# A mixer of sparse and latent attention: group A's query projections between the heads of group B, the top-k block after block, index products and ropes in PSUM

## The chip, the cores and the metric

The kernel runs on one core of one Trainium2 chip. The metric is device time in microseconds of one launch. The core's engines are TensorE (PE), VectorE (DVE), ScalarE (ACT), GpSimd (POOL) and SyncE (SP), which issues the DMAs.

## What is computed

One decoder layer on 512 tokens of 1024 numbers, all in float32:

```python
x = x + 0.5 * swiglu(rmsnorm(x, g_ffn1), w1_gate, w1_up, w1_down)      # 1024 -> 2816 -> 1024
h = rmsnorm(x, g_mix)
qa, ka, va, qi, ki, wi, cq, ckv, kr = split(h @ w_in)
qa, ka, qi, ki = (rope(t) for t in (qa, ka, qi, ki))                   # kr and part of q likewise, below
# group A: an index of 16 heads scores every causal key, each query keeps 128
score = sum over h of wi[:, h] * relu(qi[:, h] @ ki.T)                 # causal
out_a = softmax(qa @ ka.T / 8 over the 128 best keys by score) @ va    # 8 heads, one shared key and value
# group B: latent attention, 8 heads, dense and causal
q = rmsnorm(cq, g_q_lat) @ w_uq; k, v = split(rmsnorm(ckv, g_kv_lat) @ w_ukv)
out_b = softmax(q @ [k, rope(kr)].T / sqrt(96)) @ v
x = x + concat(out_a, out_b) @ w_out
x = x + 0.5 * swiglu(rmsnorm(x, g_ffn2), w2_gate, w2_up, w2_down)
return rmsnorm(x, g_final)
```

## The kernel before

Every matmul that needs float32 is three: `mm3` (L135) multiplies the high part of the weights by the high and the low part of the data, and the low part of the weights by the high one (L137, L140, L141). `split` (L93) makes the parts: ACT copies the high one (L94), DVE or POOL subtracts it for the low one (L95). The two feed-forward layers use this with 128x512 tiles; they and their code stay as they are.

Between them stands `mixer` (L574). Tokens of the string `ORDER` (L27) name its steps, and the steps run in the string's order. Ahead of the bar come `q0` to `q7` (index query projections), `s` (their rope and the stack of four rows of high and low parts for the index product), `i0` to `i7` (two index heads each), `l0` to `l4` (the latents, with their norm), `K`, `R`, `V` (keys and values of group B), `p`, `u` (rotary queries of B), `A0` to `A3` with `S0` to `S3` (query projections of group A with rope and stack) and `b3` and the like (three rounds of the top-k). Behind the bar a unit of attention is four tokens: `g` gathers its operands, `s` makes the scores and the softmax, `z` divides by the sums, `a` transposes the probabilities and multiplies them by the values. Units 0 to 7 are the heads of B, 8 to 15 a query block of A each for two groups of four heads. `o0` to `o7` are the output projection. A second table, `ON_VECTOR` (L32), names the operations that go to DVE rather than POOL (`engine`, L395). The scheduler of the language orders each engine's instructions from this, by the operands' readiness.

What the steps issue:

- `rope` (L622) reads a projection from PSUM: DVE multiplies by the cosine (L626); the sine half is either two more on DVE (L628, L629) or an ACT copy (L632) and two on POOL (L633, L634); the sum is L635. The operands of all but the first are in SBUF. `stack` (L644) then copies to SBUF (L648, L650) and subtracts (L649).
- `index_heads` (L700): for each query block of 256, 384 and 512 keys two matmuls (L707, L708) into a PSUM bank, a relu by ACT into an SBUF tile r, four of which exist (L710), and DVE's multiply-add of r into the score tile `idx` (L711).
- `topk` (L715): 16 rounds; in each, for each of the three blocks, MAX8 (L719) finds the eight largest and MATCH_REPLACE (L720) overwrites them. At the end the taken are made a mask (L723).
- `softmax` (L862): DVE adds the mask and takes the maximum out of PSUM (L872), prepares the bias (L876, L878), ACT exponentiates (L880); `normalise` (L883) is a reciprocal (L887) and a product, on POOL (L890) or DVE (L892). The probabilities of a unit lie in one of three tiles.
- `Mla` (L910) for a head of B: scores L942 to L944, transposes L957, copies out of PSUM (L906 DVE, L908 ACT, in `taken`), values L960. `Dsa` (L965) does the same for A: L982, L983, L993, L998.
- All PSUM tiles come from one pool of eight banks (`ps`, L73). Transposed blocks have seven SBUF buffers (`ah=7`).

```python
for i in range(1, NT):                                    # L715, in each of 16 rounds
    m8 = small(8)
    nc.vector.max(out=m8, in_=score[i])
    nc.vector.match_replace(out=score[i], in_to_replace=m8, in_values=score[i], imm_value=TAKEN)
```

Of the kernel before, what the change touches and what calls it, by code (L numbers as in the profile page):

```python
# [25 lines left out]
BUFS = dict(pf=5, pr=4, ph=2, ah=7)  # L26
ORDER = """q0 q1 T c s0 r s1 t k q2 v w q3 i0 q4 a s2 i1 s4 q6 i2 q7 s3 q5 s6 s7 e s5 i3 l0 i4 i7 l1 i5 i6 l2 l3 l4 p b3 n0 u A0  # L27
A1 b2 K S0 A2 R b2 b2 S1 b2 A3 b3 S3 V S2 |
g0 s0 n1 g1 b2 g2 b2 s1 z0 s2 z1 b2 g3 g4 a0 s3 a1 b2 g5 z2 s4 a2 b2 z4 g6 z3 s5 g7 a3 s6 g8 z5 b2 b2 g9 a4 s7 g10 a5
b2 z6 s8 b2 a6 b2 b2 z7 a7 s9 o0 z8 g11 b2 b2 g12 b20 z9 b2 s10 z10 a8 s11 a9 a10 z11 g13 s12 o1 a11 g14 s13 z12 g15  # L30
s14 z13 s15 a12 z14 b2 o2 a13 a14 z15 a15 o3 o4 o5 b2 b2 o6 b2 o7 b2"""
ON_VECTOR = set("""c0.0 c0.1 c0.2 c0.3 c1.0 c1.2 c10.0 c11.0 c13.0 c14.3 c15.0 c15.1 c15.3 c2.1 c2.3 c3.1 c3.2 c3.3 c4.0 c4.3  # L32
c5.1 c6.0 c6.1 c6.2 c6.3 c7.2 gk5 gk7 kf mrA2 mrT mre mrq1 mrq2 mrq3 mrq5 mrq7 oa00 oa01 oa02 oa10 oa20 oa23
oa31 oa32 oa33 ob1 ob2 re rq1 rq2 rq3 rq5 ru1 sA2 sq6 sq7 su1 wA3 wV wl0 wl3 wo0 wo1 wo4 wo5 wo6 wo7 wq1 wq2
wq5 wq6 wq7 z0.0 z0.2 z0.3 z10.0 z10.2 z11.2 z12.0 z12.2 z12.3 z13.0 z13.2 z14.2 z14.3 z15.0 z15.1 z15.2 z2.3
z3.0 z3.1 z3.2 z3.3 z4.2 z4.3 z5.1 z5.2 z6.0 z6.2 z7.0 z7.1 z7.2 z7.3 z8.0 z9.0 z9.1""".split())
# [4 lines left out]
class Kernel:  # L41
    def __init__(self, ctx, tc):
# [8 lines left out]
        self.psp = pool("psp", space=bass.MemoryType.PSUM)  # L51
# [343 lines left out]
def engine(nc, name):  # L395

    return nc.vector if name in ON_VECTOR else nc.gpsimd


def add_mixer_weights(k, w_in, w_uq, w_ukv, w_out):  # L400
# [9 lines left out]
    lo = lambda name: engine(nc, "w" + name)  # L410
# [27 lines left out]
    def rope_chunk(col, *names):  # L438
# [25 lines left out]
    def plain(col, *names):  # L464
# [48 lines left out]
    def prep_pe():  # L513
        h, l = k.whl()
        for c in range(2):
            for half in range(2):
                hv, lv = (x[:, :768].rearrange("p (a g s h b) -> p a g s h b", a=3, g=2, s=2, h=4)[:, :, c, half]
                          for x in (h, l))
                k.split(hv, lv, uq[c][:, :, :, 64 + 16 * half:80 + 16 * half], lo("p"))
        return tuple(x[:, :768].rearrange("p (a g b) -> p a g b", a=3, g=2) for x in (h, l))  # L520

    def prep_nope(c):
        def f():
            h, l = k.whl()
            hv, lv = (x[:, :768].rearrange("p (a h b) -> p a h b", a=3, h=4) for x in (h, l))
            k.split(hv, lv, uq[c][:, :, :, 0:64], lo(f"n{c}"))
# [12 lines left out]
    for part in (1, 0):  # L539
        for half in range(2):  # L540
# [692 lines left out]
```

## Time and profile before

| | |
|---|---|
| device time, median of 3 runs | 1060.51 us (1060.31 to 1060.97) |
| the profiled execution's own time | 1061.52 us |
| its span in the trace | 1059.7 us |
| mean granted clock of PE | 0.987 |
| PE busy | 1016.4 us, 96% of the span |
| DVE busy | 513.2 us, 48% |
| ACT busy | 384.3 us, 36% |
| POOL busy | 147.5 us, 14% |

Busy time is the time in which an engine had an instruction in work. The shares are means over stages that differ: the feed-forward layers fill PE, the mixer in between, some 290 us of 1060, doesn't. The granted clock is the share of full speed that PE was given. A wait belongs to the engine that stands still; it is put down to the instruction that ended it last.

### The profile page before, as it was taken

The page shows a single profiled execution, that of the slowest core. Times are in us where ns is not written, and L with a number is a line of the kernel's source. Part 1 is how long each engine was busy: PE and PEld are TensorE (multiplying, and loading weights), DVE is VectorE, ACT ScalarE, POOL GpSimd, SP SyncE. Part 2 cuts the span into 40 slices and gives each one's busy share as a digit, 9 for nine tenths or more (in the row PEclk, how much of TensorE's full clock was granted, in tenths as well). Part 3 has the DMA queues.
Part 4 walks back from the last instruction along what each step waited for, and adds up shares of the span by engine and source line. Part 5 has one row for each costly group of instructions (what it writes and reads, how often), then busy time and mean ns, then how long its engine had stood idle before and what let it go on. Part 6 is the DMA issues. An engine that isn't in the chain of part 4 may idle for free.

```text
span 1059.7 us, 12214 instructions
## 1 busy us (share of the span) xinstructions
PE 1016.4 (96%) x4726; PEld 829.8 (78%) x4726; DVE 513.2 (48%) x897; ACT 384.3 (36%) x689; POOL 147.5 (14%) x142
## 2 busy tenths in 40 slices
PE   6999999999999999889879999999999999999997
PEld 4888888888888888768755567888888888888886
DVE  6433333233332346989996767553333233333343
ACT  5422222122222335563466556442222211222232
POOL 1000000000000026625975122000000000000000
PEclk9999999999999999989988999999999999999999
DMA  8322332233313123333350001344323232222302
GB/s 278 120 80 81 118 119 80 80 99 109 111 60 97 40 80 109 114 92 98 98 174 15 2 19 43 102 138 124 113 80 119 80 113 86 80 83 98 119 0 80
DMA packets 83390, 98.84 MB, mean 93 GB/s; under 512 B 9026, under 2 KB 65474, under 8 KB 83332
## 3 DMA queue, kind: packets, MB, share of 16 engines
q1 hardware_dynamic: 83328, 98.06, 29.4%
q8 instruction: 37, 0.61, 0.2%
q14 instruction: 21, 0.17, 0.1%
q10 hardware_dynamic: 4, 0.00, 0.0%
HBM read 91.89 MB, written 2.10 MB: 89 GB/s over the span
## 4 chain that ended last, share of the span: by engine, by line
PE 80%; DVE 12%; issue 3%; ACT 3%; POOL 1%; DMA 1%; SPq 0%; POOLq 0%; ACTq 0%; DVEq 0%
PE ps L137 24%; PE ps L140 24%; PE ps L141 24%; DVE idx L720 2%; DVE s L719 2%; DVE idx L711 1%; PE ps L960 1%; DVE wl L95 1%; PE ps L998 1%; DVE p L892 1%; PE ps L993 1%; PE ps L957 1%; DVE p L872 1%; PE ps L982 1%; DVE f L626 0%
## 5 line engine op out<-in xcount | busy, mean ns | idle before, releaser
L94 ACT ACTIVATE wh<-raw 128x1024 fp32r<-128x1024 f32 (+4 forms) x154 | 140.1, 925 | 381.1 <-PE ps L140 298.9
L95 DVE TENSOR_TENSOR wl<-raw,wh 128x1024 fp32r<-128x1024 f32 (+1 forms) x122 | 145.5, 1196 | 266.2 <-ACT wh L94 265.9
L137 PE MATMUL ps<-xh,wh 128*128 128x512 f32 (+2 forms) x712 | 265.9, 378 | 5.1 <-DVE res L1137 1.7
L141 PE MATMUL ps<-xh,wl 128*128 128x512 f32 (+2 forms) x712 | 267.3, 377 | 1.2 <-POOL wl L95 0.9
L140 PE MATMUL ps<-xh,wh 128*128 128x512 f32 (+2 forms) x712 | 267.2, 377 | 0.5 <-DVE xh L95 0.5
L137 PEld LDWEIGHTS ps<-xh,wh 128*128 128x128 f32 x712 | 133.7, 189 | 29.6 <-DVE f L629 2.1
L141 PEld LDWEIGHTS ps<-xh,wl 128*128 128x128 f32 x712 | 134.6, 189 | 24.9 <-POOL wl L95 1.3
L140 PEld LDWEIGHTS ps<-xh,wh 128*128 128x128 f32 x712 | 134.5, 189 | 23.6 <-DVE xh L95 0.7
L137 PE MATMUL ps<-wh,h 128*128 128x512 f32 x272 | 105.9, 389 | 0.0
L140 PE MATMUL ps<-wl,h 128*128 128x512 f32 x272 | 105.8, 389 | 0.0
L141 PE MATMUL ps<-wh,h 128*128 128x512 f32 x272 | 105.8, 389 | 0.0
L95 POOL TENSOR_TENSOR wl<-raw,wh 128x512 fp32r<-128x512 f32 (+5 forms) x32 | 43.3, 1374 | 394.4 <-ACT wh L94 389.8
L334 DVE TENSOR_TENSOR t<-ps,t 128x512 f32<-128x512 f32 x44 | 30.4, 691 | 138.5 <-PE ps L141 138.5
L94 ACT ACTIVATE w<-raw 128x1024 fp32r<-128x1024 f32 x32 | 33.9, 1061 | 117.5 <-PE ps L140 117.5
L137 PE MATMUL ps<-xh,w 128*128 128x512 f32 x176 | 68.5, 389 | 0.0
L141 PE MATMUL ps<-xh,w 128*128 128x512 f32 x176 | 68.5, 389 | 0.0
L140 PE MATMUL ps<-xh,w 128*128 128x512 f32 x176 | 68.5, 389 | 0.0
L289 POOL TENSOR_TENSOR fr<-tot,mhalf 128x1 f32<-128x1 f32 x12 | 7.0, 582 | 417.9 <-DVE tot L1180 360.1
L140 PEld LDWEIGHTS ps<-wl,h 128*128 128x128 f32 x272 | 51.1, 188 | 10.6
L141 PEld LDWEIGHTS ps<-wh,h 128*128 128x128 f32 x272 | 51.1, 188 | 10.6
L137 PEld LDWEIGHTS ps<-wh,h 128*128 128x128 f32 x272 | 51.0, 188 | 10.6
L95 DVE TENSOR_TENSOR w<-raw,w 128x1024 fp32r<-128x1024 f32 x32 | 39.2, 1225 | 29.8 <-ACT w L94 29.8
(214 smaller groups left out, 1346.2 us busy)
## 6 DMA issues: line engine op xcount, KB each, us to landing
raw<-in_w_up_dram SPq DMA_DIRECT2D x22, 1024.0 KB, 5.3
raw<-in_w_gate_dram SPq DMA_DIRECT2D x21, 1024.0 KB, 5.3
raw<-in_w_down_dram SPq DMA_DIRECT2D x20, 1024.0 KB, 5.0
raw<-in_w_in_dram SPq DMA_DIRECT2D x8, 1024.0 KB, 5.2
raw<-in_w_out_dram SPq DMA_DIRECT2D x4, 1024.0 KB, 5.8
res<-in_x_dram SPq DMA_DIRECT2D x4, 512.0 KB, 6.0
raw<-in_w_down_dram SPq DMA_DIRECT2D x4, 512.0 KB, 3.8
raw<-in_w_ukv_dram SPq DMA_DIRECT2D x2, 1024.0 KB, 4.9
```

The source lines that it names most:

```text
L94: i = self.nc.scalar.activation(hi, src, AF.Copy)
L95: (lo_engine or self.nc.vector).tensor_tensor(out=lo, in0=src, in1=hi.bitcast(F32), op=ALU.subtract)
L137: i = mm(out, wh, xh, start=first, stop=False)
L140: mm(out, wh, xl, start=False, stop=False)
L141: return i, mm(out, wl, xh, start=False, stop=last)
L334: nc.vector.tensor_tensor(out=u, in0=pu, in1=g, op=ALU.mult)
L711: nc.vector.scalar_tensor_tensor(out=score[i], in0=r, scalar=wt[:, i, h:h + 1], in1=cm(i) if h == 0 else score[i], op0=ALU.mult, op1=ALU.add)
L719: nc.vector.max(out=m8, in_=score[i])
L720: nc.vector.match_replace(out=score[i], in_to_replace=m8, in_values=score[i], imm_value=TAKEN)
L872: nc.vector.tensor_tensor_reduce(out=e, in0=p[:, :n], in1=bias, scale=1.0, scalar=-3.0e38, op0=ALU.add, op1=ALU.max, accum_out=mx[:, c:c + 1])
L892: nc.vector.tensor_scalar(out=e, in0=e, scalar1=rc[:, c:c + 1], scalar2=None, op0=ALU.mult)
L957: nc.tensor.transpose(p[:, i * P:(i + 1) * P], probs[i][:, j * P:(j + 1) * P], k.ident)
```

## The change

It rewrites the mixer's order and what its steps use.

- **Order.** The tokens `A0` to `A3`, `S0` to `S3` and `V` move behind the bar, between the tokens of B's heads. The even heads 0, 2, 4 come first. `x` replaces `s` for the index stacks, `n0` begins ahead of the bar, and the top-k's tokens `b` follow the units.
- **Top-k.** All 16 rounds of the first block, then of the second, then of the third, in place of three blocks in each round.
- **Index and rope in PSUM.** The relu overwrites its PSUM bank and DVE's L698 (before: L711) reads it there; the four SBUF tiles r go. `rope` issues four instructions on DVE (L624 to L627 after), the last two overwrite the projection's bank; the stack is split from it with ACT and DVE. Only the shared rotary key's rope is given to POOL, from SBUF.
- **Low parts of the mixer's weights** are all made by POOL; `ON_VECTOR` goes. Two short lists remain, of products that go to POOL and of copies that go to DVE.
- **PSUM.** Eight banks to the bar; behind it six for scores, projections and transposes and two for the sums of values over a pair of heads (`k.long`); at `||`, ahead of `o0`, eight again.
- **SBUF.** Four sets of probabilities in place of three, in the space of tiles of the first stages; five buffers for transposed blocks in place of seven; values of B in a pool of the attention.

The core of the diff:

```diff
-ORDER = """... l2 l3 l4 p b3 n0 u A0
-A1 b2 K S0 A2 R b2 b2 S1 b2 A3 b3 S3 V S2 |
-g0 s0 n1 g1 b2 g2 b2 s1 z0 s2 z1 b2 g3 g4 a0 s3 a1 b2 g5 z2 s4 a2 b2 z4 g6 z3 s5 g7 a3 s6 g8 z5 b2 b2 g9 ..."""
+ORDER = """... l2 l3 l4 p n0 K u R | g0
+s0 A0 g2 V z0 s2 A1 S0 a0 z2 A2 a2 g4 s4 n1 A3 S2 g1 s1 z4 S1 z1 g6 S3 a1 b1 a4 g3 s3 b1 s6 g5 z3 a3 s5 b2 z6 g7 z5 s7
+a5 a6 g8 s8 z7 a7 b1 g9 || b1 s9 o0 ..."""
+SETS = (0, 1, 0, 2, 3, 1, 2, 0)
...
-    def acc(self):
-        return self.ps("ps", 8)
...
+    def psum(self, n):
...
+        tile = lambda tag, bufs: p.tile([P, 512], F32, tag=tag, name=self.name(tag), bufs=bufs)
+        self.acc = self.sc = self.tr = lambda: tile("ps", n)
+        self.long = lambda: tile("po", 8 - n)
...
-    lo = lambda name: engine(nc, "w" + name)
+    lo = nc.gpsimd
...
-    def rope(p, tab, name, n0=0):
+    def rope(p, tab, n0=0, eng=nc.vector):
         c, s = (t[:, n0:] for t in tab)
-        a, b = (f32()[:, n0:] for _ in range(2))
-        nc.vector.tensor_tensor(out=a, in0=p, in1=c, op=ALU.mult)
...
-        engine(nc, name).tensor_tensor(out=a, in0=a, in1=b, op=ALU.add)
-        return a
+        b = short()[:, n0:]
+        eng.tensor_tensor(out=b[lower], in0=p[upper], in1=s[upper], op=ALU.mult)
+        eng.tensor_tensor(out=b[upper], in0=p[lower], in1=s[lower], op=ALU.mult)
+        eng.tensor_tensor(out=p, in0=p, in1=c, op=ALU.mult)
+        eng.tensor_tensor(out=p, in0=p, in1=b, op=ALU.add)
+        return p
...
-                r = fr()[:, :n]
-                nc.scalar.activation(r, p, AF.Relu)
-                nc.vector.scalar_tensor_tensor(out=score[i], in0=r, scalar=wt[:, i, h:h + 1],
+                nc.scalar.activation(p, p, AF.Relu)
+                nc.vector.scalar_tensor_tensor(out=score[i], in0=p, scalar=wt[:, i, h:h + 1],
                                                in1=cm(i) if h == 0 else score[i], op0=ALU.mult, op1=ALU.add)
...
     def topk():
-        for _ in range(TOPK // 8):
-            for i in range(1, NT):
+        for i in range(1, NT):
+            for _ in range(TOPK // 8):
                 m8 = small(8)
                 nc.vector.max(out=m8, in_=score[i])
                 nc.vector.match_replace(out=score[i], in_to_replace=m8, in_values=score[i], imm_value=TAKEN)
-            yield
-        for i in range(1, NT):
+                yield
             nc.vector.tensor_scalar(out=score[i], in0=score[i], scalar1=TAKEN, scalar2=NEG, op0=ALU.not_equal, op1=ALU.mult)
-        yield
...
-    k.probs = lambda: ap.tile([P, 4 * T], F32, tag="p", name=k.name("p"), bufs=3)
-    turned = k.junk = lambda: ap.tile([P, T], F32, tag="h", name=k.name("h"), bufs=BUFS["ah"])
+    def turned():
+        attn.h += 1
+        return attn.pool.tile([P, T], F32, tag="h", name=k.name("h"), bufs=2) if attn.h % 5 < 2 else short()
```

How it moves the instructions. First DVE at the first rounds of the top-k, before (`idx_2657`, `idx_2658` and `idx_2659` are the scores of the three query blocks, `s` the eight largest):

```order
L720 MATCH_REPLACE idx_2657<-s_3673,idx_2657 128x256
L720 MATCH_REPLACE idx_2658<-s_3676,idx_2658 128x384
L720 MATCH_REPLACE idx_2659<-s_3679,idx_2659 128x512
L719 MAX s_3682<-idx_2657 128x8
L719 MAX s_3685<-idx_2658 128x8
L719 MAX s_3688<-idx_2659 128x8
```

and now (`idx_2659` is the first block here):

```order
L706 MAX s_4247<-idx_2659 128x8
L707 MATCH_REPLACE idx_2659<-s_4247,idx_2659 128x256
L706 MAX s_4316<-idx_2659 128x8
L707 MATCH_REPLACE idx_2659<-s_4316,idx_2659 128x256
L706 MAX s_4417<-idx_2659 128x8
L707 MATCH_REPLACE idx_2659<-s_4417,idx_2659 128x256
```

Three blocks took turns, so that an instruction and the next had different operands; now each of the first block's instructions reads what the one ahead wrote.

Second DVE at the first softmax of a head of group B (`L872` before, `L865` after; `p` are the probabilities, `ps` the scores). Before, it follows the masks that end the top-k (`L723`):

```order
L723 TENSOR_SCALAR idx_2657<-idx_2657 128x256
L723 TENSOR_SCALAR idx_2658<-idx_2658 128x384
L95 TENSOR_TENSOR wl_4184<-raw_4069,wh_4183 128x1024
L723 TENSOR_SCALAR idx_2659<-idx_2659 128x512
L872 ISA p_4173,s_4170<-ps_4155,cmask 128x128
L872 ISA s_4170 128x1
L872 ISA p_4173,s_4170<-ps_4155,cmask 128x256
L872 ISA s_4170 128x1
L872 ISA p_4173,s_4170<-ps_4162,cmask 128x384
```

and now it stands in the second block's rounds (`idx_2660`), with the rope of `A0` (`L624` on, `ps_3749`) close behind:

```order
L706 MAX s_4844<-idx_2660 128x8
L707 MATCH_REPLACE idx_2660<-s_4844,idx_2660 128x384
L865 ISA p_3733,s_3730<-ps_3715,cmask 128x128
L865 ISA s_3730 128x1
L865 ISA p_3733,s_3730<-ps_3715,cmask 128x256
L865 ISA s_3730 128x1
L865 ISA p_3733,s_3730<-ps_3722,cmask 128x384
L865 ISA s_3730 128x1
L706 MAX s_4847<-idx_2660 128x8
L865 ISA p_3733,s_3730<-ps_3726,cmask 128x512
L865 ISA s_3730 128x1
L624 TENSOR_TENSOR f_3903<-ps_3749,tab_2792 64x512
```

The first softmax moved from behind the top-k into it.

Third PE at the first scores. Before, group A's last projection (`ps_3999`) and the values of B (`ps_4075` and on) stand ahead of the first head's scores (`L942`, `ps_4155`):

```order
L137 MATMUL ps_3999<-xh_2637,wh_3819 128x512
L140 MATMUL ps_3999<-xh_2638,wh_3819 128x512
L141 MATMUL ps_3999<-xh_2637,wl_3820 128x512
L137 MATMUL ps_4075<-wh_3873,lat_3582 128x512
L137 MATMUL ps_4084<-wh_3873,lat_3582 128x512
L137 MATMUL ps_4093<-wh_3873,lat_3582 128x512
L137 MATMUL ps_4102<-wh_3873,lat_3582 128x512
L942 MATMUL ps_4155<-st_4131,st_4133 128x256
```

and now (`L941`, `L942` are the scores; `ps_3749` is the projection `A0`):

```order
L141 MATMUL ps_3689<-lat_3461,wh_3524 128x512
L142 MATMUL ps_3689<-lat_3460,wl_3525 128x512
L941 MATMUL ps_3715<-st_3701,st_3703 128x256
L942 MATMUL ps_3715<-st_3702,st_3703 128x256
L941 MATMUL ps_3722<-st_3701,st_3703 128x384
L942 MATMUL ps_3722<-st_3702,st_3703 128x384
L941 MATMUL ps_3726<-st_3701,st_3703 128x512
L942 MATMUL ps_3726<-st_3702,st_3703 128x512
L138 MATMUL ps_3749<-xh_2392,wh_3600 128x512
L141 MATMUL ps_3749<-xh_2393,wh_3600 128x512
L142 MATMUL ps_3749<-xh_2392,wl_3601 128x512
```

The scores of head 0 come ahead of group A's first projection and of the values, which now follow them.

## Rows read from the trace of the kernel before

**Rows 1.** Busy time by stage of the mixer (view of windows): start and end in us from the span's start and the length; then the busy us and, in brackets, the instructions of PE, PEld (PE's weight loads), DVE, ACT and POOL; then the granted clock of PE as a share of full speed, the share of the DMA engines' time, and GB/s.

```profile
382.00:421.00 39.00, 37.15 (x200) 34.62 (x199) 23.52 (x40) 18.92 (x40) 21.59 (x21) 0.96 0.38 120
421.00:478.00 57.00, 49.34 (x240) 42.10 (x238) 53.25 (x73) 35.02 (x73) 23.75 (x15) 0.94 0.35 101
478.00:552.00 74.00, 65.91 (x306) 52.95 (x305) 73.91 (x188) 33.94 (x56) 57.61 (x46) 0.97 0.38 117
552.00:612.00 60.00, 55.45 (x249) 33.92 (x248) 41.35 (x135) 37.69 (x108) 21.64 (x26) 0.92 0.09 27
612.00:672.00 60.00, 55.92 (x323) 41.80 (x322) 41.09 (x113) 31.54 (x85) 11.71 (x12) 1.00 0.18 59
```

**Rows 2.** Groups of DVE's instructions from 421 to 478 us, the index stage, kept apart by shape: line, engine, operation, output<-inputs with shapes, count | busy us, mean ns of one | idle us before.

```profile
L711 DVE SCALAR_TENSOR_TENSOR idx<-r,wt,idx 128x512 f32<-128x512 f32 x15 | 14.8, 985 | 0.0
L711 DVE SCALAR_TENSOR_TENSOR idx<-r,wt,idx 128x384 f32<-128x384 f32 x15 | 11.9, 796 | 0.1
L711 DVE SCALAR_TENSOR_TENSOR idx<-r,wt,idx 128x256 f32<-128x256 f32 x15 | 10.0, 667 | 0.0
L95 DVE TENSOR_TENSOR wl<-raw,wh 128x1024 fp32r<-128x1024 f32 x2 | 3.3, 1630 | 0.8 <-ACT wh L94 0.8
L626 DVE TENSOR_TENSOR f<-ps,tab 128x384 f32<-128x384 f32 x5 | 2.7, 549 | 0.0
L628 DVE TENSOR_TENSOR f<-f,tab 64x512 f32<-64x512 f32 x1 | 2.7, 2703 | 0.1
L649 DVE TENSOR_TENSOR h<-f,qst 128x384 fp32r<-128x384 f32 x2 | 1.9, 961 | 0.0
...
L95 DVE TENSOR_TENSOR wl<-raw,wh 128x512 fp32r<-128x512 f32 x2 | 1.3, 680 | 0.0
...
L626 DVE TENSOR_TENSOR f<-f,tab 128x512 f32<-128x512 f32 x1 | 0.7, 693 | 0.0
```

**Rows 3.** DVE's instructions in order of time, from 443 to 458 us: start us, duration us, line, operation, output<-inputs with shapes, count.

```profile
440.86 2.88 DVE L711 SCALAR_TENSOR_TENSOR idx<-r,wt,idx 128x512 f32<-128x512 f32 x1
...
447.45 2.70 DVE L628 TENSOR_TENSOR f<-f,tab 64x512 f32<-64x512 f32 x1
...
451.36 0.47 DVE L711 SCALAR_TENSOR_TENSOR idx<-r,wt,idx 128x256 f32<-128x256 f32 x1
...
453.62 0.62 DVE L711 SCALAR_TENSOR_TENSOR idx<-r,wt,idx 128x384 f32<-128x384 f32 x1
```

**Rows 4.** POOL's instructions in the same stretch, the same columns.

```profile
440.48 2.71 POOL L95 TENSOR_TENSOR wl<-raw,wh 128x1024 fp32r<-128x1024 f32 x1
...
446.89 2.71 POOL L95 TENSOR_TENSOR wl<-raw,wh 128x1024 fp32r<-128x1024 f32 x1
```

**Rows 5.** Groups of DVE's instructions from 478 to 552 us, the top-k stage, columns as in rows 2.

```profile
L95 DVE TENSOR_TENSOR wl<-raw,wh 128x1024 fp32r<-128x1024 f32 x3 | 5.1, 1696 | 0.0
L626 DVE TENSOR_TENSOR f<-ps,tab 128x512 f32<-128x512 f32 x6 | 4.0, 667 | 0.0
...
L742 DVE SCALAR_TENSOR_TENSOR lat<-ps,g_kv_lat,lat 128x512 fp32r<-128x512 f32 x2 | 1.5, 733 | 0.0
...
L635 DVE TENSOR_TENSOR f<-f,f 128x512 f32<-128x512 f32 x1 | 1.0, 1046 | 0.0
...
L711 DVE SCALAR_TENSOR_TENSOR idx<-r,wt,idx 128x512 f32<-128x512 f32 x1 | 0.7, 739 | 0.0
```

**Rows 6.** Pieces of the chain that ended last, from 400 to 600 us: start us, us, engine, output and line, and how many instructions follow each other.

```profile
478.72 1.38 DVE s L719 x3
480.10 1.58 DVE idx L720 x3
...
550.86 0.60 DVE p L872
```

**Rows 7.** Busy time of a slice where the top-k ends, columns as in rows 1.

```profile
540.00:560.00 20.00, 12.39 (x40) 7.42 (x39) 17.77 (x48) 14.18 (x34) 13.75 (x13) 0.78 0.33 97
```

**Rows 8.** PE's instructions in order of time, from 426 to 455 us: the first and the second index head of a pair begin in the first two rows; the last two are the first and the last of the 24 matmuls of one query projection.

```profile
429.43 0.28 PE L707 MATMUL ps<-kih,qst 128*128 128x256 f32 x1
...
430.48 0.28 PE L707 MATMUL ps<-kih,qst 128*128 128x256 f32 x1
...
431.57 0.44 PE L137 MATMUL ps<-xh,wh 128*128 128x384 f32 x1
...
435.69 0.33 PE L141 MATMUL ps<-xh,wl 128*128 128x384 f32 x1
```

**Rows 9.** What PE waited for from 421 to 672 us: engine, tile and line that waited <- engine, tile and line waited for: us in total, times, longest.

```profile
PE ps L998 <- ACT h L908: 2.3, 3, 1.0
PE ps L957 <- DVE p L892: 2.2, 2, 1.3
...
PE ps L137 <- DVE f L629: 1.6, 1, 1.6
```

**Rows 10.** DVE's instructions in order of time around 594 us, columns as in rows 3.

```profile
594.25 0.16 DVE L878 TENSOR_TENSOR s<-s,scol 128x4 f32<-128x4 f32 x1
594.33 0.17 DVE L887 RECIPROCAL s<-s 128x4 f32<-128x4 f32 x1
594.54 0.97 DVE L892 TENSOR_SCALAR p<-p,s 128x128 f32<-128x128 f32 x2
```

**Rows 11.** What ACT waited for from 421 to 478 us, columns as in rows 9.

```profile
ACT r L710 <- DVE idx L711: 9.5, 8, 3.3
```

More of the change, by code (lines that the diff above doesn't have):

```diff
@@ L50, in __init__ @@
         self.whp = pool("whp")
-        self.psp = pool("psp", space=bass.MemoryType.PSUM)
+        self.n = 0
+        self.psp = None
+        self.psum(8)
         self.n = 0
@@ L642, in quarters, with stack @@
         return [x[32 * q:32 * q + 32] for q in range(4)]
-    def stack(x, make, name, n0=0):
+    def stack(x, make, n0=0):
         out = [make()[:, n0:] for _ in range(2)]
-        l = f32r()[:, n0:]
-        nc.scalar.activation(out[0], x, AF.Copy)
-        engine(nc, name).tensor_tensor(out=l, in0=x, in1=out[0].bitcast(F32), op=ALU.subtract)
+        l = short(F32R)[:, n0:]
+        k.split(out[0], l, x)
         nc.scalar.activation(out[1], x, AF.Copy)
@@ L692, in rotary_key @@
     def rotary_key(x):
-        scaled(tk, v.rows1)
-        x = rope(x, tk, "re")
-        h, l = f32r(), f32r()
+        x = rope(x, v.tk, 0, nc.gpsimd)
+        h, l = short(F32R), short(F32R)
         k.split(h, l, x, nc.gpsimd)
@@ L781, in index_stack @@
     def index_stack(j):
-        stacks[j] = stack(rope(pq.pop(j), ta, f"rq{j}", P), qst, f"sq{j}", P)
+        stacks[j] = stack(rope(pq.pop(j), ta, P), qst, P)
     def keys_b(j):
@@ L836, in stack_a @@
     def stack_a(j):
-        qa[2 * j], qa[2 * j + 1] = stack(rope(pa.pop(j), v.ta, f"rA{j}"), mkqa, f"sA{j}")
+        qa[2 * j], qa[2 * j + 1] = stack(rope(pa.pop(j), v.ta), mkqa)
     def values_b(j):
@@ L961, in apply @@
             if odd:
[L962 to L963 removed]
+                oT[4 + pr] = k.xh(), k.xl()
+                k.split(*oT[4 + pr], Mla.po.pop(pr))
     class Dsa:
@@ L1017, in out_part @@
             out_done(t, half, p, part == 0)
-    do = dict(g=lambda j: units[j].gather(), s=lambda j: units[j].score(), z=lambda j: normalise(j),
-              a=lambda j: units[j].apply(), o=out_part, n=lambda j: k.weights(ids[f"n{j}"]), b=background)
-    for w in steps[steps.index("|") + 1:]:
+    do = dict(T=keys, c=norm_column, t=rest, r=norm_rows, k=index_keys, v=rest_out, w=lambda j: values(v.x2),
+              e=lambda j: rotary_key(v.x2), q=index_queries, i=lambda j: index_heads(j, stacks.pop(j)), l=latent,
+              K=keys_b, R=keys_b_out, p=rotary_b, u=rotary_b_out, n=lambda j: k.weights(ids[f"n{j}"]), A=queries_a,
+              S=stack_a, V=values_b, b=background, x=index_stack,
+              g=lambda j: units[j].gather(), s=lambda j: units[j].score(), z=lambda j: normalise(j),
+              a=lambda j: units[j].apply(), o=out_part)
+    for w in steps:
+        if w == "||":
+            k.psum(8)
+            continue
+        if w == "|":
+            k.psum(6)
+            proj_scope.close()
+            attn.pool = mix.enter_context(k.tc.tile_pool(name="attn", bufs=1, reuse_waits="tile"))
+            continue
         do[w[0]](int(w[1:] or 0))
```

186 lines of the change are left out of this document (89 added, 97 removed).

## The prediction

> **What bounds the kernel now.** I read busy time by stage first, then the groups of one engine in one stage, and only then single stretches. TensorE (PE) is busy nearly throughout the two feed-forward layers, which the change leaves alone; what there is to gain lies in the mixer, 382 to some 672 us [rows 1]. PE is idle there for 7.7 of the 57 us in which the index is summed (421 to 478), for 8.1 of 74 us in the top-k (478 to 552), and for 8.6 of the 120 us behind. VectorE (DVE) is busy 53.3 of those 57 and 73.9 of those 74 us. So from 421 to 552 us **DVE ends the stage**, and PE's idle time is what DVE leaves.
>
> In the index stage DVE's time is the sum over the index heads, L711, 15 instructions each at 256, 384 and 512 columns, of 667, 796 and 985 ns on the mean [rows 2]. Single ones take 0.47 and 0.62 us [rows 3], and one behind the stage 739 ns [rows 5]. The long ones lie beside POOL: an L711 of 2.88 us beside a POOL instruction of 2.71, an L628 with two SBUF operands of 2.70 beside another of 2.71 [rows 3, 4]. Instructions that read PSUM are not stretched: L626 takes 549 ns at 384 columns, and L742, a form like L711's, 733 ns at 512, in stretches where POOL worked [rows 2, 5]. In the top-k the three query blocks of a round cost 1.38 us of MAX8 and 1.58 us of replacement, 2.96 us; 16 rounds make 47.4 us, and the first softmax of a head begins only at 550.86 us [rows 6]. By then PE has used up its projections: from 540 to 560 us it is busy 12.39 of 20 us at a granted clock of 0.78 [rows 7].
>
> **The change, part by part.** The sum is made against the profiled execution's own 1061.5 us; the median of the runs is 1.0 us lower.
>
> *Before the index sum, 382 to 421 us.* PE is busy 37.15 of 39 us at a clock of 0.96 [rows 1], so idle time gives at most 1.9. The key ropes come wholly to DVE and the weights' lo parts go to POOL, which can move the first index product either way. **-1**, ends -3 and +2.
>
> *Index stage, 57 us before.* DVE's 53.3 us change as follows. L711 (L698 after) reads its product from PSUM. At 0.47, 0.62 and 0.74 us instead of the means it saves 15 x (0.197 + 0.176 + 0.245) = 9.3 [rows 2, 3, 5]. The rotary key goes to POOL: its L628 of 2.70 and three more of some 0.69 [rows 2], 4.8 less. The weights' lo parts go to POOL: 3.3 + 1.3 = 4.6 less [rows 2]. The five query ropes of this stage, 13 DVE instructions and some on POOL before, become 20 of 0.55 us: 7 more, 3.9. The lo parts of five stacks, 0.55 each, replace two of 1.9 together: 0.9 more. Left are 53.3 - 9.3 - 4.8 - 4.6 + 3.9 + 0.9 = 39.4 us. Then PE ends the stage: its 49.3 us at a clock of 0.94 are 46 at full clock [rows 1]. With 2 us of waits I take 48, **-9**. The lower end is -12 (no gap, no low clock); the upper is +3, for banks that run short.
>
> No row has L711's form on PSUM beside POOL: its saving lies between 0 (as now) and 9.3 (as L742), and L742 is the nearest in form.
>
> The relu now overwrites its bank, so a bank is held until L698 has read it. From one index head's first product to the next head's PE takes 1.05 us, and 24 projection matmuls 4.5 us [rows 8]. For a pair of heads with one projection PE thus needs 4.5 + 2.1 = 6.6 us, and DVE 2 x 1.83 for the sums, 2.2 for the rope and 0.55 for the stack, 6.4. That is near balance, and eight banks (six products, two projections) even it out; hence the 2 us of waits.
>
> Now PE waits once, 1.6 us, for a rope to free a bank (L629) [rows 9]. The Trainium skill speaks against this part: "PSUM — Partial Sum Buffer", section "Summary: rules for kernel authors", asks that PSUM be evacuated promptly, and the change lets two engines work in a bank before it is free. By that rule the stage's 9 us would be lost, 1059; by this trace, where one such wait is seen, they are kept.
>
> *Top-k and the first heads, 478 to 571 us.* The same 48 MAX8 and 48 replacements run block after block, so each needs the result of the one ahead. What such a link costs: L887 starts 0.08 us after an L878 of 0.16 us that it does not need, while L892, which needs L887 (0.17 us), starts 0.21 us after it [rows 10]. An independent neighbour so starts 0.08 us before the other's end, a dependent one 0.04 behind it: 0.12, say 0.11 us a link. By the order 60 of the 96 links have nothing between them: 6.6 us. Ends: 0, and 96 x 0.17 = 16 us, a whole further short instruction at each link.
>
> Between the rounds now stand softmaxes and ropes. DVE's list from the last index sum to the last mask, start to start (durations less 0.08): rounds 47.4, links 6.6, four softmaxes of B heads 6.5, eleven normalisations 3.6, six ropes of four at 0.65 (L626: 0.667 [rows 5]) 15.6, twelve lo parts at 0.6 7.3, four key products 2.4, latents 2.0, masks 1.0, small ones 2.4, in all 94.8 us. Before it was 72 us, and only then came the first softmax. That now stands 41 us into the list, with group A's projections and V beside the heads, so PE has work where it went idle at 540. What PE had done by 571 us, 93 us behind the last index sum, it has done after about 94, when DVE's list ends: **+1**. Ends: -6, if the stretched ones of this stage (L635 1046 ns for 0.68, lo parts of 1696 for 1.22 [rows 5]) go and PE is not held by the last rounds; +10 with links of 16 us.
>
> *The other heads, 571 to 672 us.* PE is idle 8.6 of 120 us [rows 1]. DVE has a quarter of the softmaxes, and the ropes, behind it; four sets of probabilities in place of three let softmaxes run ahead. Against that stand six banks for eight, and five buffers for seven for the transposed blocks. **-2**, ends -10 (all idle time, and some low clock) and +9: the 4.5 us that PE waits now for probabilities and transposed blocks [rows 9], once more, and again the low clock of 552 to 612 us (0.08 x 60).
>
> *Costed at nothing*: the lo parts of all weights on POOL. It is busy 23.8 of 57 and 57.6 of 74 us [rows 1] and loses ropes and splits in exchange; prefetching hides it. Without that cover each late one costs a matmul 1 to 2.6 us, within the ends.
>
> Sum: -1 - 9 + 1 - 2 = -11; 1061.5 - 11 = 1050.5, as a median 1049.5. I say **1050**.
>
> **The rivals.**
> - *Banks run out (slower).* ACT waits 9.5 us now until L711 frees one of its SBUF buffers [rows 11], and PE's banks are free meanwhile. Held in the bank, this becomes PE's wait. It decides when L698 keeps L711's present means: 2 x (0.667 + 0.796 + 0.985) = 4.9 us for a pair, 7.7 with rope and stack, against PE's 6.6. Price: the 9 us lost and 9.5 more, 1050 + 18.5 = 1068. Against it: PSUM readers are not stretched. Chance 0.16. The skill's rule named above is the reason that it isn't smaller.
> - *Links at their upper price (no gain).* 16 for 6.6 us, on DVE's list, which ends the stage: 1050 + 10 = 1060. It decides from 0.17 us a link. For it: the new order has next to no other work between them in the last block. Against it: the 0.11 of the rows. Chance 0.21, of which faster 0.05, same 0.07, slower 0.09.
> - *Fillers close every hole (much faster).* PE's 7.6 idle us of 540 to 560 [rows 7] and most of the 8.6 behind go too: 1050 - 14 = 1036. Chance 0.13.
> - *It doesn't do what it says*: not open, the order shows softmaxes between rounds.
>
> **How the numbers follow.** The forecast has the remaining 0.50, with a range of its own of 1041 to 1060. A measurement of this kernel can tell about 0.2%, 2.1 us, from no change. Faster: 0.45 of the forecast, 0.05, 0.13: 0.63. Same: 0.04 and 0.07: 0.11. Slower: 0.16, 0.09 and 0.01 of the forecast: 0.26. The range leaves out about a tenth on each side: 1034 to 1068.
>
> **What would show it.** L698 of 470, 605 and 740 ns without long ones; the index stage 48 us long; the first softmax about 41 us after the last L698 and the last mask about 95 after it; a replacement starting 0.04 us behind its MAX8's end; PE busy 18 or more of each 20 us up to there. It would be wrong if PE waited several us for banks at the index products, the projections or the transposes, or stood idle over 10 us before the last round.

## The result, and the profile after

The changed kernel takes **1067.06 us** (median of 4 runs, 1066.66 to 1067.88) against 1060.69 us (4 runs, 1060.31 to 1060.97): a ratio of 1.0059, 95% interval 1.0047 to 1.0072. It is 6.4 us slower; 1050 was forecast. The profiled execution has a span of 1066.1 us, at a mean granted clock of 0.987 as before.

The busy time of the whole program, from the page (engine, us, share of the span, instructions):

```profile
PE 1015.3 (95%) x4726; PEld 830.8 (78%) x4726; DVE 505.2 (47%) x919; ACT 381.8 (36%) x693; POOL 119.8 (11%) x105
```

DVE, ACT and POOL all do less than before, PE 1.1 us less. What grew is PE's idle time: 1066.1 - 1015.3 = 50.8 us, from 1059.7 - 1016.4 = 43.3. The stages show where (columns as in rows 1; the bounds follow the changed kernel's own stages):

```profile
382.00:415.00 33.00, 33.00 (x186) 30.79 (x185) 22.11 (x37) 19.42 (x41) 19.63 (x20) 1.00 0.36 112
415.00:467.00 52.00, 48.66 (x246) 41.83 (x246) 40.97 (x76) 32.81 (x71) 24.22 (x15) 1.00 0.38 112
467.00:555.00 88.00, 81.22 (x380) 64.16 (x378) 84.41 (x218) 41.24 (x83) 34.28 (x27) 0.98 0.30 94
555.00:566.00 11.00, 0.56 (x3) 0.23 (x2) 10.85 (x23) 7.05 (x16) 8.60 (x6) 0.74 0.40 126
566.00:606.00 40.00, 34.28 (x159) 20.89 (x159) 26.11 (x81) 22.57 (x65) 6.46 (x7) 0.94 0.06 14
606.00:669.00 63.00, 55.47 (x315) 40.50 (x313) 39.29 (x130) 30.00 (x87) 10.86 (x9) 0.97 0.08 26
```

Up to 555 us it goes much as forecast. The index sum starts at 415 instead of 421 us, its stage has 3.3 idle us of PE and not 7.7 [rows 1], the clock stays at 1.00. Then PE stands still for 10.4 of 11 us, and behind that it is idle for 5.7 + 7.5 us. The index stage's DVE groups (columns as in rows 2):

```profile
L698 DVE SCALAR_TENSOR_TENSOR idx<-ps,wt,idx 128x512 f32<-128x512 f32 x15 | 11.1, 743 | 0.4 <-ACT ps L697 0.4
L698 DVE SCALAR_TENSOR_TENSOR idx<-ps,wt,idx 128x384 f32<-128x384 f32 x15 | 9.1, 609 | 0.0
L698 DVE SCALAR_TENSOR_TENSOR idx<-ps,wt,idx 128x256 f32<-128x256 f32 x15 | 7.2, 477 | 0.8 <-ACT ps L697 0.6
```

These answer to the 985, 796 and 667 ns of [rows 2]: 9.3 us saved. PE's waits from 380 to 690 us (columns as in rows 9):

```profile
PE ps L956 <- DVE xh L885: 13.9, 4, 10.4
PE ps L997 <- ACT f L909: 4.6, 4, 2.5
PE ps L138 <- DVE s L865: 2.6, 1, 2.6
PE ps L695 <- DVE idx L698: 1.2, 2, 0.6
```

One more at the start of the second feed-forward layer, from 664 to 710 us:

```profile
PE ps L318 <- DVE p L304: 1.9, 2, 1.6
```

Banks cost next to nothing in the index stage (L695 for L698, 1.2 us). The large wait is that of transposes (L956) for the normalisation of their probabilities (L885), those of the fourth head in the order. PE around it, in order of time (start us, duration us, line, operation, in brackets the idle time ahead and what ended it):

```profile
554.96 0.39 PE L142 MATMUL ps<-lat,wl 128*128 128x512 f32 x1
565.79 2.37 PE L956 MATMUL ps<-ident,xh 128*128 128x128 f32 x10 [10.44 <-DVE xh L885]
```

And DVE in that hole, the same columns; `xh` holds the waited-for head's probabilities:

```profile
553.87 0.69 DVE L865 CUSTOM_DVE_ANT_0 xh<-ps,cmask 128x512 f32<-128x512 f32 x1
...
554.49 0.69 DVE L706 MAX8 s<-idx 128x8 f32<-128x512 f32 x1
555.09 0.67 DVE L96 TENSOR_TENSOR f<-ps,qa 128x512 fp32r<-128x512 f32 x1
555.79 0.69 DVE L624 TENSOR_TENSOR f<-ps,tab 64x512 f32<-64x512 f32 x1
556.50 0.68 DVE L625 TENSOR_TENSOR f<-ps,tab 64x512 f32<-64x512 f32 x1
557.22 1.00 DVE L871 TENSOR_TENSOR s<-s,scol 128x4 f32<-128x4 f32 x1
...
560.94 0.68 DVE L627 TENSOR_TENSOR ps<-ps,f 128x512 f32<-128x512 f32 x1
561.53 1.41 DVE L885 TENSOR_SCALAR p<-p,s 128x128 f32<-128x128 f32 x2
...
563.52 0.16 DVE L880 RECIPROCAL s<-s 128x4 f32<-128x4 f32 x1
563.61 0.65 DVE L96 TENSOR_TENSOR st<-ps,st 64x512 fp32r<-64x512 f32 x1
564.18 0.67 DVE L96 TENSOR_TENSOR f<-ps,qa 128x512 fp32r<-128x512 f32 x1
564.78 0.67 DVE L706 MAX8 s<-idx 128x8 f32<-128x512 f32 x1
565.38 0.85 DVE L885 TENSOR_SCALAR xh<-xh,s 128x128 f32<-128x128 f32 x3
```

The head's maximum is there at 554.5 us. Its bias (L871) then stands behind a MAX8, a stack's split and half a rope, 2.7 us; ACT exponentiates from 558.25 to 560.9; the product (L885) follows at 565.38, behind a rope's end, another head's product, a replacement, two splits and a MAX8, 4.5 us. PE had 0.56 us of work in it. So the hole of the kernel before, in its slice from 540 to 560 us [rows 7], comes back later and deeper.

A second measure of the same: each matmul from 382 us on is counted at the median time for its width from its start to the next one's (227 ns at 512 columns, 174 at 384, some 118 at 256, 109 at 128), and the times are compared at which the two kernels reach the same sum. The changed kernel is 11 us ahead at 70 us of work, some 18 at 150 (about 553 against 571 us), some 2 at 170 (about 599 against 601), and behind from 200 on, by 3 to 6. **Nearly the whole lead is lost between 553 and 599 us**, among the heads of group B.

### The profile page after: what moved, and what is told of

Its sections match the earlier page's. It is cut to its first block, busy times and chain, and to the rows that moved or that the text cites. A ratio compares the mean times of both kernels' runs of the same rounds, so it can differ in the third digit from the quotient of the medians.

```text
span 1066.1 us, 12148 instructions
## 1 busy us (share of the span) xinstructions
PE 1015.3 (95%) x4726; PEld 830.8 (78%) x4726; DVE 505.2 (47%) x919; ACT 381.8 (36%) x693; POOL 119.8 (11%) x105
## 4 chain that ended last, share of the span: by engine, by line
PE 82%; DVE 11%; ACT 3%; issue 2%; POOL 1%; DMA 1%; ACTq 0%; POOLq 0%; DVEq 0%
PE ps L138 25%; PE ps L141 25%; PE ps L142 25%; DVE idx L707 2%; DVE s L706 2%; PE po L959 1%; PE ps L992 1%; PE ps L997 1%; PE ps L956 1%; ACT wh L95 1%; DVE p L865 1%; DVE st L96 1%; PE ps L981 1%; DVE f L625 0%; DVE p L885 0%
## 5 line engine op out<-in xcount | busy, mean ns | idle before, releaser
L96 DVE TENSOR_TENSOR wl<-raw,wh 128x1024 fp32r<-128x1024 f32 (+1 forms) x102 | 122.7, 1204 | 264.4 <-ACT wh L95 264.1
L96 POOL TENSOR_TENSOR wl<-raw,wh 128x512 fp32r<-128x512 f32 (+5 forms) x52 | 76.1, 1486 | 455.0 <-ACT wh L95 450.7
L142 PEld LDWEIGHTS ps<-wh,h 128*128 128x128 f32 x272 | 51.0, 188 | 10.7
```

Source lines behind the costliest of these rows:

```text
L96: (lo_engine or self.nc.vector).tensor_tensor(out=lo, in0=src, in1=hi.bitcast(F32), op=ALU.subtract)
L142: return i, mm(out, wl, xh, start=False, stop=last)
```

## The experiments

All ratios are to the kernel before, timed beside each, with 95% intervals. "The heads' stretch" is the time from the third softmax of B, with six heads to go, to A's first.

**One part of the changed kernel undone.** Three causes were at hand: the links between rounds, DVE's longer list, the banks.

e1_turns lets the blocks take turns again; e2_half_on_pool gives the sine products of group A's ropes and of B's rotary queries to POOL; e4_eight_banks takes one pool of eight banks throughout; e3_before_serial is the kernel before with block after block, its tokens `b` spread as they were:

```diff
 e1
-        for i in range(1, NT):
-            for _ in range(TOPK // 8):
+        for _ in range(TOPK // 8):
+            for i in range(1, NT):
 e2, in rope
+            nc.scalar.activation(x, p, AF.Copy)
+            nc.gpsimd.tensor_tensor(out=b[lower], in0=x[upper], in1=s[upper], op=ALU.mult)
+            nc.gpsimd.tensor_tensor(out=b[upper], in0=x[lower], in1=s[lower], op=ALU.mult)
 e4
-            k.psum(6)
+            k.psum(8)
-        self.long = lambda: tile("po", 8 - n)
+        self.long = lambda: tile("po", 8 - n) if n < 8 else tile("ps", n)
 e3
-        for _ in range(TOPK // 8):
-            for i in range(1, NT):
+        for i in range(1, NT):
+            for _ in range(TOPK // 8):
...
+                n += 1
+                if n % 3 == 0:
+                    yield
```

> The changed kernel with the top-k's three blocks taking turns again in each round. Theory L (the time is set by DVE's list between the last index sum and the fifth softmax, which got 17 us longer: 8 of links, 9 and more of ropes): the links go, 48 MAX8 and 48 replacements fall from 55.5 to 47.5 us of start-to-start time, the fifth softmax starts 5 to 8 us earlier, 1059 to 1062 us. Rival M (six PSUM banks and five buffers for transposed blocks slow the heads): no change, 1066 to 1068. The scheduler puts the first softmax later among the rounds (behind 40 of 48 in place of 28), which could cost some of it under either.

> The changed kernel with the sine half of six ropes (four of group A, two of B's rotary queries) on POOL again, from a copy by ACT. Theory L: twelve DVE instructions of 0.68 us leave its list, 8 us, less what POOL's work stretches; 1059 to 1063 us. Rival M: no change or slower, since the copies take from the same three SBUF tiles as the transposed blocks; 1067 to 1070.

> The changed kernel with one pool of eight PSUM banks behind the bar in place of six and two. Theory L: no change within 1.5 us, 1065.5 to 1068.5. Rival M: the heads get faster, 1064 or less.

> The kernel before with its top-k block after block, nothing else. Theory L: its DVE is busy without a gap from 421 to 552 us, so the links' 8 us come through nearly whole: 1065 to 1069 us. Rival M, by which the links don't matter: 1060 to 1062.

Measured: e1 1080.4 us, 1.0188 [1.0172, 1.0203]; e2 1073.9, 1.0130 [1.0107, 1.0152]; e4 1075.5, 1.0144 [1.0128, 1.0159]; e3 1063.3, 1.0030 [1.0017, 1.0042]. Neither theory had any of these times. Each undone part makes the changed kernel slower still, and the serial rounds cost the old kernel only 2.6 us. None of the three alone brings the time back. The hole stays, at 5.5 us in e2 and nearly whole in the other two: PE's waits from 500 to 606 us, first of e1 and then of e4.

```profile
PE ps L958 <- DVE xh L887: 11.6, 2, 9.4
```

```profile
PE ps L956 <- DVE xh L885: 14.1, 4, 10.7
PE ps L959 <- ACT h L909: 10.9, 2, 9.9
```

9.4 and 10.7 us on the same normalisation. In e4 a second wait of 9.9 us appears: values of a head for their transposed blocks.

**The last block's rounds later, the projections back.** f1_third_after_z1 and f2_third_after_z5 hold the third block's rounds until the last product of unit 1 or 5 (`v.hold`); f4_order_back has the projections of A ahead of the bar again; f3_index_alone is the kernel before with the index's relu and sum in PSUM and nothing else:

```diff
 f1, f2
-                nc.vector.max(out=m8, in_=score[i])
+                m = nc.vector.max(out=m8, in_=score[i])
+                if i == 3 and v.hold:
+                    k.after(m, v.hold)
 f4
-l4 p n0 K u R | g0 s0 A0 g2 V z0 s2 A1 S0 a0 z2 A2 a2 g4 s4 n1 A3 S2 g1 s1 z4 S1 z1 g6 S3 a1 b1
+l4 p n0 u A0 A1 K S0 A2 R S1 A3 S3 S2 | V g0 s0 g2 z0 s2 a0 z2 a2 g4 s4 n1 g1 s1 z4 z1 g6 a1 b1
 f3
-                nc.scalar.activation(r, p, AF.Relu)
+                nc.scalar.activation(p, p, AF.Relu)
-                nc.vector.scalar_tensor_tensor(out=score[i], in0=r, scalar=wt[:, i, h:h + 1],
+                nc.vector.scalar_tensor_tensor(out=score[i], in0=p, scalar=wt[:, i, h:h + 1],
```

> The changed kernel with one order more: the third block's rounds on DVE come behind the last normalisation of head 1 (L885), the fourth unit in order. Nothing is removed. Theory Q (in DVE's queue rounds and ropes stand ahead of the short instructions of heads 4 and 1, 18 us from softmax to transposes, and PE, out of projections, waits 10.4 us for them): that wait falls under 4 us, the fifth softmax starts 6 to 12 us earlier than 575.6 and the time is 1053 to 1062 us. Theory L (the sum of DVE's work ends the mixer): the work only moves, 1065 to 1069 us.

> The same with the third block's rounds behind the normalisation of head 5. Theory Q: the heads come earlier still, but the third block is needed for the 13th unit's softmax, and its 16 rounds of some 1.5 us, 24 us, now have to fit between the heads' end and that: 1050 to 1062 us. Theory L: 1065 to 1069 us.

> The changed kernel with the order's main part undone: group A's projections and stacks ahead of the bar again, the rest as changed. Theory Q: group A's ropes no longer stand among the heads, but the first softmax comes behind 43 of 48 MAX8, so that PE runs out of work as in the kernel before; 1060 to 1067 us. If the new order by itself loses the time: 1050 to 1056 us. Theory L: 1065 to 1069 us.

> The kernel before with one part of the change: the relu overwrites its PSUM bank and the sum over index heads reads it there. Both theories: the sums are 9 us shorter, DVE is busy without a gap to 552, so the top-k begins and ends 5 to 9 us earlier; 1051 to 1057 us. Rival B (a bank held longer makes PE wait, or the gain is lost in the heads as in the changed kernel): 1059 to 1068 us.

Measured: f1 1073.1, 1.0118 [1.0103, 1.0133]; f2 1075.3, 1.0145 [1.0128, 1.0162]; f4 1087.7, 1.0252 [1.0236, 1.0267]; **f3 1053.6, 0.9934 [0.9919, 0.9948]**. f1 and f2 still wait 8.4 us at a time for the normalisation, so the last rounds are not what holds it. f3 beats both kernels: the index part is worth 7.1 us alone. Its first two softmaxes begin 7 us earlier than before (549.75 and 551.58 us there):

```profile
542.47 0.28 DVE L871 CUSTOM_DVE_ANT_0 p<-ps,cmask 128x128 f32<-128x128 f32 x1
544.86 0.28 DVE L871 CUSTOM_DVE_ANT_0 p<-ps,cmask 128x128 f32<-128x128 f32 x1
```

In f4 PE waits once for 14.6 us (500 to 606 us): ropes that work in their banks hold them, and the next projection has none.

```profile
PE ps L138 <- ACT qa L641: 14.6, 1, 14.6
PE ps L956 <- DVE xh L885: 12.2, 2, 9.9
```

**From the other side, part by part onto f3.**

```diff
 g1, to f3
-    lo = lambda name: engine(nc, "w" + name)
+    lo = lambda name: nc.gpsimd
 g2, to f3: rope, b holding two products of p, all on DVE
+        eng.tensor_tensor(out=p, in0=p, in1=c, op=ALU.mult)
+        eng.tensor_tensor(out=p, in0=p, in1=b, op=ALU.add)
```

g2_index_ropes also gives the stacks and the low parts of A's keys to ACT and DVE, and the rotary key's rope to POOL, as the change does. Before, DVE's own sine products (L628, L629) already read a projection in PSUM; new is that the cosine product and the sum are written back to it. g3_index_ropes_lo is g1 and g2 together. g4_all_but_order is g3 with e3's loops, h3_index_serial f3 with them.

> A ladder from the kernel before to the changed one, on top of the relu in PSUM (1053.6 us). This step: the low parts of all the mixer's weights on POOL. Theory S (what loses the time is the new order with its pools, not the single parts): 1051 to 1056 us. Theory R (the ropes in place lose it): the same. If POOL's work stretches DVE's instructions with two SBUF operands enough: 1058 us or more.

> The relu in PSUM and all ropes in place in PSUM on DVE, stacks split from there, the rotary key's rope on POOL; order, top-k, weights and pools as before. Theory R (a projection's bank is held until four rope instructions and three copies of its stack are done, and DVE has two more instructions for a rope): 1058 to 1066 us. Theory S: 1050 to 1056 us.

> The last two steps together on top of the relu in PSUM. Theory R: 1058 to 1066 us. Theory S: 1050 to 1057 us.

> As the last, and the top-k block after block: every part of the change but the order of group A's projections, the pools of PSUM and the sets of probabilities. Theory R: 1061 to 1069 us, the changed kernel's 1067 is reached or nearly so. Theory S: 1052 to 1059 us, and what is missing to 1067 belongs to the order and the pools.

> The kernel before with the relu in PSUM (1053.6 us alone) and the top-k block after block (2.6 us slower alone, 1.3 us faster on top of the ropes and low parts). If DVE's links count where DVE is bound: 1055 to 1058 us. If the rounds then only fill gaps: 1051 to 1054 us.

| | us | ratio | step |
|---|---|---|---|
| f3, index alone | 1053.6 | 0.9934 [0.9919, 0.9948] | -7.1 to before |
| g1, and low parts on POOL | 1060.0 | 0.9999 [0.9989, 1.0008] | +6.4 to f3 |
| g2, and ropes in PSUM | 1065.2 | 1.0045 [1.0030, 1.0060] | +11.5 to f3 |
| g3, both | 1060.4 | 0.9997 [0.9988, 1.0006] | +6.8 to f3 |
| h3, and block after block | 1061.6 | 1.0009 [1.0000, 1.0018] | +7.9 to f3 |
| g4, g3 and block after block | 1059.1 | 0.9983 [0.9974, 0.9992] | -1.3 to g3 |
| the changed kernel | 1067.1 | 1.0059 [1.0047, 1.0072] | +8.0 to g4 |

The parts don't add up: ropes and low parts cost 11.5 and 6.4 us alone and 6.8 together, serial rounds 7.9 on f3 and nothing on g3 (the intervals of g3 and g4 overlap). But two steps stand. The index gain is nearly used up by low parts, ropes and rounds together (g4 is 1.6 us under before), and what g4 lacks costs 8.0 us more: the new order, its pools and sets, but also the two short lists of products and copies, and the split of each head's queries, which POOL made before and DVE makes in the changed kernel.

For g1 the trace names the queue. POOL, the same columns as above, first in g1 and then in f3:

```profile
536.20 2.51 POOL L95 TENSOR_TENSOR wl<-raw,wh 128x1024 fp32r<-128x1024 f32 x1
538.67 1.26 POOL L635 TENSOR_TENSOR f<-f,f 128x512 f32<-128x512 f32 x1
540.01 1.26 POOL L95 TENSOR_TENSOR xh<-kf,xh 64x512 fp32r<-64x512 f32 x1
```

```profile
534.30 1.27 POOL L95 TENSOR_TENSOR xh<-kf,xh 64x512 fp32r<-64x512 f32 x1
```

The low part of the second head's keys (`xh<-kf`) starts 5.7 us later, behind a weight's low part of 2.51 us; POOL has no gap from 504 to 552 us. PE's waits for that head and for the third (`st`), in g1 (480 to 560 us):

```profile
PE ps L941 <- DMA xh<-pe: 4.6, 1, 4.6
PE ps L943 <- POOL st L95: 3.1, 1, 3.1
```

In f3 the first of them is 1.8 us, and the stack of the third costs 1.4 and 0.5. The profiled run of g1 is 4.2 us behind f3's: 2.1 of them are lost at these heads, the other 2.1 only at the start of the second feed-forward layer; what the medians differ by beyond that is open. For g2 it is DVE first. Its top-k stage, columns as in rows 1:

```profile
473.00:549.00 76.00, 67.24 (x311) 55.79 (x309) 75.57 (x183) 29.46 (x49) 31.01 (x27) 0.92 0.38 113
```

and one of PE's waits from 380 to 560 us:

```profile
PE ps L137 <- DVE idx L703: 5.9, 3, 2.9
```

DVE is busy 75.57 of 76 us, and the last mask comes 16.9 us later than in f3 (555.72 against 538.86 us). The 5.9 us lie in the index stage: three projections wait there for banks that index products hold until DVE has summed them (L703), the shortage that the prediction's rival described.

**The place of the seventh head and of A's stacks.** In the order, of `z0 s2 A1 S0 a0 z2 A2 a2 g4 s4 n1 A3 S2 g1 s1 z4 S1 z1 g6 S3 a1 b1 a4 g3 s3 b1 s6 g5` these became:

```diff
 h1_s6_ahead
+g4 s4 n1 A3 S2 g1 s1 z4 S1 z1 g6 s6 S3 a1 b1 a4 g3 s3 b1 g5
 h2_stacks_behind
+g4 s4 n1 A3 z4 S2 g1 s1 z1 S1 g6 s6 S3 a1 b1 a4 g3 s3 b1 g5
 h4_stacks_early
+z0 s2 A1 S0 a0 z2 S1 A2 a2 S2 g4 s4 n1 A3 z4 S3 g1 s1 z1 g6 s6 a1 b1 a4 g3 s3 b1 g5
```

> The changed kernel with one token moved: the scores of head 6 ahead of the transposes of heads 1 and 4. Theory P (heads 4 and 1 are a pair, nothing of a later head stands in PE's order between their scores and their transposes, so their whole chain of softmax, exponential and division, 14 to 18 us, shows as PE's wait): head 6's softmax starts by 563 in place of 575.6 us, the wait of 10.4 us at 555 shrinks to under 8, the time is 1057 to 1063 us. If what holds the pair is DVE's list, as the sum of its work: 1065 to 1069 us.

> As that, and the division of head 4 ahead of group A's next rope, the divisions of heads 4 and 1 ahead of its other two. Theory P: 2 to 4 us less than the last one, 1054 to 1061 us. DVE's list: 1065 to 1069 us.

> As that, and three of group A's stacks one head earlier than in the changed kernel, so that no rope stands behind head 1's scores. Theory P: 1052 to 1060 us. DVE's list: 1065 to 1069 us, since the same work stands ahead of the fifth softmax.

Measured: h1 1067.3, 1.0062 [1.0045, 1.0078]; h2 1067.3, 1.0061 [1.0041, 1.0082]; h4 1079.1, 1.0176 [1.0154, 1.0198]. h1 fills part of the hole: its fifth softmax starts at 567.28 us, not 575.61, and PE's wait becomes one of 6.9 us for another head's stack. But its end is the same: the 8.3 us of the fifth softmax are 2.7 at the eighth (591.10 against 593.77 us) and 1.5 at A's first. Filling the hole alone gains nothing, and these places are not the cause.

**Sixteen rounds less.** i1_after_two_blocks and i2_before_two_blocks drop the first block's 16 rounds from the changed kernel and from the kernel before, so that they compute another mask:

```diff
 i1
-            for _ in range(TOPK // 8):
+            for _ in range(TOPK // 8 if i > 1 else 0):
 i2
-            for i in range(1, NT):
+            for i in range(2, NT):
```

> The changed kernel without the 16 rounds of the first query block (its mask is then made from untouched scores): DVE's work between the last index sum and group A's first softmax gets some 15 us less (16 times 0.46 + 0.08 + 0.44), and no step of a head changes. Theory L (the sum of DVE's work up to group A's first softmax sets the time, wherever in the stretch it stands): 1051 to 1057 us. Theory C (the heads' own chain through the engines' queues sets it): 1062 us or more.

> The kernel before without the same 16 rounds, 0.73 us each without links, 11.7 us. Theory L: 1048 to 1053 us. Theory C: 1056 us or more.

Measured: i1 1071.2, 1.0093 [1.0077, 1.0109]; i2 1054.1, 0.9933 [0.9916, 0.9949]. Without 16 rounds DVE is busy 12.7 us less in the old order and the kernel gains 6.6 us. In the new order DVE is busy 11 us less from the last sum to A's first softmax (107 us for 118) and the kernel is 4 us *slower* than the changed one. Its last mask is made at 538.0 us in place of 570.0, and still PE waits 9.2 us at a time for the same normalisation (500 to 606 us):

```profile
PE ps L956 <- DVE xh L885: 12.7, 4, 9.2
```

So the hole needs no round of the top-k in DVE's queue. The heads of i1 (columns as in rows 1):

```profile
555.00:603.00 48.00, 31.00 (x129) 18.78 (x130) 25.74 (x79) 27.55 (x73) 11.47 (x10) 0.82 0.13 35
```

PE is idle for 17 of 48 us, and DVE, ACT and POOL each for 20 us and more: no engine's load ends this stretch, waits of one engine for another do.

The heads' stretch in all orders, in us for each of its six heads. Old order: i2 6.7, f3, g1, g3 and h3 6.8, before and e3 6.9, g4 7.0, g2 7.2. New order: changed 8.6, e1 8.0, f4 8.1, h1 8.3, f2 8.8, h2 8.9 and i1 8.9, f1 9.7, e2, e4 and h4 9.8. Nothing that was tried brings the new order near 7.

What part of the new order does it is **open**. Rounds (f1, f2, i1), banks (e4), the stacks' and the seventh head's places (f4, h1, h2, h4) leave the pace as it is or worsen it. Not tried apart: the even heads first, five buffers for transposed blocks, four sets of probabilities, the two short lists, the queries' split on DVE, the sums over a pair of heads in banks of their own (only with e4). One caution holds for all runs on the changed kernel: the scheduler also reorders other instructions (in f1, where only rounds on DVE are held, PE's order changes too), so that a slower run shows less than a hole that stays.

## Why the prediction was wrong

- **Before the index sum, -1: more.** PE is busy all of the 33 us, and the sum starts 6.3 us earlier. The lower end was -3.
- **Index stage, -9: right in kind.** Means of 477, 609 and 743 ns were forecast as 470, 605 and 740, with none long; the stage takes 51.6 us for 57.1 where I took 48. PE ends it, as forecast, but is busy in it for 48.7 us where I took 46, and idle for 3.3 where I took 2. Alone it is worth 7.1 us. The Trainium skill's rule that the prediction weighed ("PSUM — Partial Sum Buffer", "Summary: rules for kernel authors": evacuate promptly) would have lost this; here PE waits 1.8 us in all for L698, so this trace doesn't bear it out. Other runs do: PE waits 14.6 us in f4 for banks held by ropes, and 5.9 us in g2 for banks held by index products.
- **Links, 6.6 us: right.** A dependent instruction starts 0.034 us behind the end of the one ahead, an independent one 0.077 before it: the 0.11 of the forecast. Of the 96 links 55 have nothing between them (60 forecast). The rounds take 8 us more by DVE's list, 2.6 in time on the kernel before (e3).
- **"PE has work where it went idle at 540 ... +1": the step that failed.** From start to start the first softmax comes 42.9 us behind the last sum (41 forecast), the last mask 103.9 behind it (95). The step set DVE's list against PE's progress by 571 us, as if PE could take any work as long as the list ran. PE takes its own in its order. It had reached that work at 553 us and stood at one head's transposes, whose probabilities DVE finished 10.4 us later. The prediction's own sign of being wrong, over 10 idle us of PE before the last round, thus came true: the hole ends at 565.8 us, the last replacement begins at 569.25. From the last sum to A's first softmax it is 132.9 us, 117.9 before: 15 us where I had +1 and, for the heads behind, a share of -2. The length of DVE's list is not what sets this: in i1 DVE has 11 us less to do in the stretch, and it takes 137.0. What in the new order does is open.
- **"The other heads -2": wrong in sign.** From the third softmax to A's first PE is idle 15.9 of 52 us, in the kernel before 3.7 of 42:

```profile
547.00:599.00 52.00, 36.14 (x170) 24.33 (x169) 40.88 (x116) 29.96 (x76) 15.42 (x12) 0.90 0.17 46
```

```profile
554.00:596.00 42.00, 38.26 (x180) 24.27 (x178) 32.01 (x94) 27.95 (x75) 19.33 (x21) 0.91 0.10 30
```

  Four sets of probabilities did not let softmaxes run ahead there: with six heads to go in both, the stretch takes 51.7 us where before takes 41.4, 10.3 of the 15 us above.
- **"Costed at nothing: the lo parts of all weights on POOL": wrong.** On f3 it costs 6.4 us. I priced a late weight, not what stands behind a weight in POOL's queue: in g1 the low parts of the second head's keys and of the third's stack. Some 2 us go only at the start of the second feed-forward layer, in the changed kernel (L318's wait above) and in g1 alike.
- **The rivals.** Neither slower one happened in the changed kernel. The banks did not run out at its index products (they do, for 5.9 us, in g2), and the links kept to their price. The time lies in the range given, near its upper end, by a way that none of them named.

## What to carry to other kernels

A list of one engine's work that fits into the time is not yet a schedule: find the instruction at which the next engine stands in order, and count what lies ahead of its supplier in that supplier's queue. A move that fills a hole early can push it to the next place where a producer's queue is shared, as here from 540 to 555 us and, in h1, on to another head's stack. When a bundle is slower, try its parts alone on the old kernel: here three lines of it (f3) were worth 7.1 us, and the rest of the bundle lost them and 6.4 more.

## What the runs showed of the hardware

A DVE multiply-add with one operand in PSUM and one in SBUF is not stretched beside a busy POOL: 743 ns at 512 columns with POOL busy 24 of 52 us, and 985 with both in SBUF [rows 2], single ones up to 2.88 us [rows 3]. The Trainium skill ("SBUF — State Buffer", "Who interferes with whom") says that a DVE instruction with at most one SBUF input, outside its two-port modes, doesn't contend with GpSimd, and that one with two does when GpSimd reads SBUF; the traces agree, f3's means of 741, 606 and 474 ns too.

Dependent neighbours on DVE, in the last block's rounds of the changed kernel:

```profile
536.52 0.69 DVE L706 MAX8 s<-idx 128x8 f32<-128x512 f32 x1
537.25 0.09 DVE L707 MATCH_VALUE_LOAD idx<-s,idx 128x8 f32 x1
537.33 0.68 DVE L707 MATCH_REPLACE8 idx<-s,idx 128x512 f32<-128x512 f32 x1
538.04 0.69 DVE L706 MAX8 s<-idx 128x8 f32<-128x512 f32 x1
```

The load starts 0.04 us behind MAX8's end, the next MAX8 0.03 behind the replacement's.

TensorE's granted clock was 1.00 through the 85 us ahead of the top-k, 0.98 to 555 us and 0.74 in the 11 us in which PE stood still, between its levels of 1.2 and 2.4 GHz; the 40 us behind had 0.94.
